# A chunked recurrence beside dense projections: TensorE's order written by the kernel, and an inverse by blocks of 16 in place of 32

## The chip, the cores and the metric

The kernel runs on one core of a Trainium2 chip. The metric is the device time of one execution in microseconds (us), as the median of several runs. A core has TensorE (PE, which multiplies matrices; its weight loads are shown apart as PEld), VectorE (DVE), ScalarE (ACT), GpSimd (POOL) and SyncE (SP, which issues the transfers). Each works through its own list of instructions in order, and semaphores make one wait for another.

## The reference, cut to what matters

The model is a streaming encoder of two layers with D = 1024. It takes 1024 frames of a new stream and 64 frames of a running one. Layer 1 mixes over time with RWKV-7, layer 2 with attention over a sliding window; each is followed by a SwiGLU feed-forward part (FFN). The change lies in the RWKV-7 part, a recurrence with a 64x64 state in each of 16 heads:

```
def step(s, inp):
    r_t, w_t, k_t, v_t, a_t, b_t = inp
    sa = jnp.einsum('bhvk,bhk->bhv', s, a_t)
    s = s * w_t[:, :, None, :] + sa[..., None] * b_t[:, :, None, :] + v_t[..., None] * k_t[:, :, None, :]
    return s, jnp.einsum('bhvk,bhk->bhv', s, r_t)
...
s_fin, y = lax.scan(step, s0.astype(f32), seq_in)
```

After the scan y is normalised per head, a bonus is added, the gate is multiplied in, and the result is projected by w_o. Everything is float32.

## The kernel before

**Tiling.** Tokens are cut into half A (512 frames) and half B (512 frames and the 64 of the running stream, 576 to 580 columns). Features lie on the 128 partitions, 8 tiles of 128. A dense product is made three times over from a high and a low part of each operand: `Dense.mm` (L433 to L435, tile dp) issues high x high, high x low and low x high for each of 8 tiles of the contraction. Weights come in pieces of 512 columns (tile wr); ACT makes the high part (wh, L393), DVE or POOL the low part (wl, L394).

**The recurrence.** It runs in chunks of 64 frames, 17 in all: chunks 0 to 7 beside the r, k and v projections of half B (called stage 1 here), chunks 8 to 16 beside the output projection of half A and its first FFN (stage 2). Both stages are one call of `recur`, the second followed by one for chunk 16. A chunk has four parts, in class `Rwkv`:

- `prep` loads r, k, a and the log decay s, makes scaled copies AR and BK on DVE, ACT and POOL, the norms of the keys (p_rp from c_bd, then tile r_n), the four *triangle groups* (p_rp from r_AR and r_BK, masked by DVE into X, named r_G, L152), and the bonus (tile r_vf).
- `prep2` inverts a triangular 64x64 matrix per head (`inverse`), then copies the rest of X and transposes BK (tile r_BT).
- `chain` is what goes from chunk to chunk: U0 (p_rc from r_sv and r_G), copied by ACT (L283); U (p_rc from r_yc and W), copied by DVE and ACT (L287, L288); the new state (p_rc from r_sv and r_BT, then DVE L301 and L302, tile r_M); and the output Y (p_ry, from r_M and r_AR, then from r_sv and r_G).
- `post` normalises Y, transposes it and stores it (scratch z).

**The inverse.** The 64x64 triangle of each head is seen as two blocks of 32 on the diagonal. ACT copies the diagonal blocks four times over into one tile (L190, 32x1024), so that DVE can solve all heads at once with a row per lane: `for j in range(30, 0, -2)` multiplies (L215) and adds (L219), in up to two halves per step. The two blocks are then joined on TensorE by two groups of 32x32 matmuls (p_rc from r_ixd and r_in, and p_rc from r_ixd alone), each followed by a copy in two halves (L246 on ACT and L247 on DVE; L253 and L254). The result is W, a single buffer.

**What sets the order.** All instructions are handed to a scheduler, which replays them on a model timeline and gives each engine its list. A priority decides between instructions that are ready (low number first). `Two.at(pe, rest)` gives the recurrence's matmuls one priority and its other work another:

```
def recur(chunks, M, base, low):
    rw.two.at(base, base)
    d = rw.prep(chunks[0])
    rw.prep2(d)
    for i, ch in enumerate(chunks):
        ...
            rw.two.at(base + 0.301 + late, low + 0.301 + late)
            nd = rw.prep(chunks[i + 1])
        rw.two.at(base + late, base + late)
        M, Y = rw.chain(ch, d, M)
```

So TensorE's list is the scheduler's. The triangle groups of chunk i+1 come ahead of the chain of chunk i, and its inverse follows behind it.

## Time and profile before

| what | us |
|---|---|
| median of 3 runs | 3048.13 (3044.47 to 3050.98) |
| the profiled execution | 3042.33 |
| its span, from the first to the last instruction | 3040.6 |
| TensorE busy in it | 2854.4 (94%) |
| VectorE busy | 1885.7 (62%) |
| ScalarE busy | 1371.7 (45%) |
| GpSimd busy | 920.5 (30%) |

The profile comes from one execution. Its page gives busy time by engine, the same in 40 slices of 76 us, the clock that TensorE was granted, and the costliest groups of instructions. Views of the trace cut this further: by window, by line, by wait, or in order of time. A float32 matmul of the recurrence that the kernel issues once stands in the trace twice, so "x32" there is 16 of the program. Stage 1 lies at about 265 to 690 us of the span, stage 2 at about 690 to 1192 us.

### The profile page before, as it was taken

The page shows a single profiled execution, that of the slowest core. Times are in us where ns is not written, and L with a number is a line of the kernel's source. Part 1 is how long each engine was busy: PE and PEld are TensorE (multiplying, and loading weights), DVE is VectorE, ACT ScalarE, POOL GpSimd, SP SyncE. Part 2 cuts the span into 40 slices and gives each one's busy share as a digit, 9 for nine tenths or more (in the row PEclk, how much of TensorE's full clock was granted, in tenths as well). Part 3 has the DMA queues.
Part 4 walks back from the last instruction along what each step waited for, and adds up shares of the span by engine and source line. Part 5 has one row for each costly group of instructions (what it writes and reads, how often), then busy time and mean ns, then how long its engine had stood idle before and what let it go on. Part 6 is the DMA issues. An engine that isn't in the chain of part 4 may idle for free. (4 is left out here: it accounts for less than half of the span.)

```text
span 3040.6 us, 51529 instructions
## 1 busy us (share of the span) xinstructions
PE 2854.4 (94%) x19650; PEld 2463.5 (81%) x19650; DVE 1885.7 (62%) x3964; ACT 1371.7 (45%) x2491; POOL 920.5 (30%) x785
## 2 busy tenths in 40 slices
PE   6998888988899999999999999999999999999998
PEld 5677777876677777887789999888777888999998
DVE  8887788968998994357554333565554335533334
ACT  6866665545545542244653222344554233322222
POOL 6555124333333332224211222243111222322221
PEclk9999778988899999999999999999999999999999
DMA  4645353344232225332212222222222332322222
GB/s 145 169 124 148 112 144 93 108 118 133 78 95 88 89 69 137 100 114 80 70 49 63 84 84 84 77 85 79 65 67 74 94 94 80 105 84 84 84 84 70
DMA packets 262048, 289.10 MB, mean 95 GB/s; under 512 B 125029, under 2 KB 143973, under 8 KB 261801
## 3 DMA queue, kind: packets, MB, share of 16 engines
q1 hardware_dynamic: 261800, 285.81, 31.7%
q8 instruction: 154, 2.52, 0.4%
q14 instruction: 94, 0.76, 0.1%
HBM read 243.18 MB, written 41.16 MB: 94 GB/s over the span
## 5 line engine op out<-in xcount | busy, mean ns | idle before, releaser
L433 PE MATMUL dp<-xh,wh 128*128 128x288 f32 (+2 forms) x3480 | 1180.3, 340 | 29.2 <-DVE hx L962 11.4
L434 PE MATMUL dp<-xl,wh 128*128 128x288 f32 (+2 forms) x3480 | 1172.0, 337 | 9.7 <-POOL xl L426 6.5
L435 PE MATMUL dp<-xh,wl 128*128 128x288 f32 (+2 forms) x3480 | 1167.9, 336 | 0.0
L393 ACT CAST wh<-wr 128x512 fp32r<-128x512 f32 x730 | 446.0, 619 | 820.4 <-PE dp L434 613.5
L433 PEld LDWEIGHTS dp<-xh,wh 128*128 128x128 f32 x3480 | 665.6, 192 | 109.9 <-DVE hx L962 16.0
L434 PEld LDWEIGHTS dp<-xl,wh 128*128 128x128 f32 x3480 | 666.0, 191 | 74.6 <-issue 8.6
L435 PEld LDWEIGHTS dp<-xh,wl 128*128 128x128 f32 x3480 | 666.2, 191 | 60.3 <-issue 4.9
L394 POOL TENSOR_TENSOR wl<-wr,wh 128x512 fp32r<-128x512 f32 x243 | 340.2, 1400 | 1063.2 <-ACT wh L393 948.7
L394 DVE TENSOR_TENSOR wl<-wr,wh 128x512 fp32r<-128x512 f32 x487 | 374.6, 772 | 421.1 <-ACT wh L393 417.0
L433 PE MATMUL dp<-mh,wh 128*128 128x288 f32 (+1 forms) x808 | 254.5, 315 | 0.2 <-DVE hx L962 0.2
L435 PE MATMUL dp<-mh,wl 128*128 128x288 f32 (+1 forms) x808 | 254.0, 314 | 0.0
L434 PE MATMUL dp<-ml,wh 128*128 128x288 f32 (+1 forms) x808 | 253.8, 314 | 0.0
L962 DVE TENSOR_TENSOR a_xB<-dp,a_xB 128x288 f32<-128x288 f32 x352 | 157.7, 455 | 83.5 <-PE dp L435 82.8
L943 DVE TENSOR_TENSOR st<-st,dp 128x288 f32<-128x288 f32 (+1 forms) x132 | 70.0, 530 | 222.0 <-PE dp L435 221.6
L945 POOL TENSOR_TENSOR xl<-st,xh 128x288 fp32r<-128x288 f32 (+1 forms) x102 | 102.2, 1002 | 327.6 <-ACT xh L944 318.8
L433 PEld LDWEIGHTS dp<-mh,wh 128*128 128x128 f32 x808 | 152.5, 189 | 10.7 <-issue 3.0
L435 PEld LDWEIGHTS dp<-mh,wl 128*128 128x128 f32 x808 | 152.6, 189 | 8.5 <-issue 2.4
L434 PEld LDWEIGHTS dp<-ml,wh 128*128 128x128 f32 x808 | 152.6, 189 | 6.8 <-issue 1.1
L190 ACT COPY r_f<-r_G 32x1024 f32<-32x1024 f32 x68 | 135.8, 1997 | 37.4 <-DVE r_f L226 25.4
L962 DVE TENSOR_TENSOR hx<-dp,hx 128x512 f32<-128x512 f32 x176 | 119.7, 685 | 47.9 <-PE dp L435 47.3
L215 DVE TENSOR_TENSOR r_f<-r_f,r_f 128x60 f32<-128x60 f32 (+5 forms) x476 | 119.4, 282 | 0.5
L944 ACT CAST xh<-st 128x288 fp32r<-128x288 f32 (+1 forms) x102 | 50.2, 492 | 137.3 <-DVE st L943 136.3
(343 smaller groups left out, 3850.3 us busy)
## 6 DMA issues: line engine op xcount, KB each, us to landing
wr<-in_ffn_in SPq DMA_DIRECT2D x352, 256.0 KB
wr<-in_ffn_out SPq DMA_DIRECT2D x176, 256.0 KB
wr<-in_rkv SPq DMA_DIRECT2D x90, 256.0 KB
wr<-in_rwo SPq DMA_DIRECT2D x32, 256.0 KB
wr<-in_wq SPq DMA_DIRECT2D x32, 256.0 KB
wr<-in_wo SPq DMA_DIRECT2D x32, 256.0 KB
r_r_s<-s_s SPq DMA_DIRECT2D x17, 256.0 KB
r_sv<-s_vt SPq DMA_DIRECT2D x17, 256.0 KB
```

The source lines that it names most:

```text
L190: S.copy(st[32 * q:32 * q + 32].rearrange("p (t g j) -> p t g j", g=4, j=8), src)
L215: V.tensor_tensor(out=Z[:, h, 1:3, r0:4, 0:j], in0=Z[:, h, a, r0:4, j:j + 2].rearrange("p r c -> p c r").unsqueeze(3).broadcast_to([128, 2 ...
L393: nc.scalar.copy(h, x)
L394: (nc.gpsimd if self.turn % 3 == 0 else nc.vector).tensor_tensor(out=l, in0=x, in1=h, op=ALU.subtract)
L433: self.nc.tensor.matmul(ps, lhsT=wh, rhs=xh, start=i == 0, stop=False)
L434: self.nc.tensor.matmul(ps, lhsT=wh, rhs=xl, start=False, stop=False)
L435: self.nc.tensor.matmul(ps, lhsT=wl, rhs=xh, start=False, stop=i == last)
L943: V.tensor_tensor(out=t[o], in0=t[o], in1=p, op=ALU.mult)
L944: S.copy(a.hi[:, q], t[o])
L945: G.tensor_tensor(out=a.lo[:, q], in0=t[o], in1=a.hi[:, q], op=ALU.subtract)
L962: V.tensor_tensor(out=self.x[m][:, q], in0=p, in1=self.x[m][:, q], op=ALU.add)
```

## The change

**TensorE's order.** A new class `Pump` holds the recurrence as a generator. Between `start` and `end` TensorE's list is the order in which the program is written. `Dense.mm` calls `tick` behind each triple of dense matmuls with their columns; `tick` takes 0.44 ns per column and 6 ns from a need, and when the need is used up the next step of the recurrence is issued. Each step yields how much dense work (in ns) is to stand before the next. `burst(6)` issues six steps without dense work between, ahead of the input mixes of r and of k; `drain` issues what is left. The lists of the other engines are still the scheduler's.

**Two chunks ahead.** `prep`, `inverse`, `chain` and `post` are now generators. In `recur`, chunk i's chain is followed by `turns`: the triangle groups, bonus and BK transposes of chunk i+2 alternate with the joins of chunk i+1's inverse.

**Blocks of 16.** The solve on DVE runs `for j in range(14, 0, -2)`, 7 steps in place of 15 and one half in place of two. The copies that spread the blocks are 32x512 in place of 32x1024. Two groups of joins are added on TensorE that make blocks of 32 out of blocks of 16 (p_rc from r_ixd, 32 matmuls of 32x16 each in the program), with a copy on ACT behind the first (L311, tile Q) and an add and a transpose on DVE behind the second (L318, L297). The joins from 32 to 64 stay, 16 matmuls each. W is now written whole, by DVE (L320) and ACT (L321).

```
-        for j in range(30, 0, -2):
+        for j in range(14, 0, -2):
...
-            part = [(h, (j // 4 + 1 - h) // 2) for h in range(2) if (j // 4 + 1 - h) // 2 < 4]
-            for h, r0 in part:
+            r0, n = j // 2, 8 - j // 2
+            V.tensor_tensor(out=Z[:, 1:3, r0:8, 0:j],
...
+            V.tensor_reduce(out=Z[:, b, r0:8, 0:j], in_=Z[:, min(a, 1):min(a, 1) + 3, r0:8, 0:j].rearrange("p c r j -> p r j c"),
+                            axis=AX.X, op=ALU.add)
...
+        for j in range(8):
+            for q in range(4):
+                o = slice(32 * q, 32 * q + 32)
+                self.mm(ps[o, j, :], lhsT=T(q, j, slice(o.start % 64, o.start % 64 + 32)), rhs=XD[o, j, 0:16], start=True, stop=True)
+        S.copy(Q1[:, :, 0:16], ps)
+        yield
...
+                self.mm(ps[o, j, :], lhsT=Q1[o, j, :], rhs=WD[o, j, 16:32], start=True, stop=True)
+        V.tensor_tensor(out=WD[:, :, 16:32], in0=ps, in1=WD[:, :, 16:32], op=ALU.add)
+        turn()
+        V.tensor_scalar(out=W[:, :, 0:32], in0=WD, scalar1=self.e[:, 2:3], scalar2=None, op0=ALU.mult)
+        S.activation(W[:, :, 32:64], WD, AF.Copy, scale=self.e[:, 3:4])
...
+    def tick(self, n):
+
+        if self.gen is None:
+            return
+        self.need -= 0.44 * n + 6
+        while self.gen is not None and self.need <= 0:
+            self.step()
...
+        def turns(g, v, p):
+
+            for gap in (1.2, 1.4, 1.2, 1.4):
+                for x in (g, v):
+                    if x:
+                        step(x, p)
+                        yield gap * scale * us
...
+            k = rw.chain(ch, ds[i], M)
+            step(k, base)
+            if g:
+                step(g, inv)
+            yield 1.8 * scale * us
...
+    pump.start(recur(range(8), M, 1, 2, *FREE[0], {7: lambda M: state.append(M)}), 1)
...
 go(rkv("B", "v", xs["Bv"]), chain(wait(3), take(8 - 3, stage)))
+    pump.burst(6)
     all(r)
     go(rkv("B", "r", xs["Br"]), chain(stage, several(2, take(RING - 8, k))))
+    pump.burst(6)
     all(k)
     all(rkv("B", "k", xs["Bk"]))
-    prio(3)
-    M = recur(range(8, 16), M, 3, LOW[1])
...
+    pump.drain()
...
+    pump.start(recur(range(8, 17), state[0], 3, 4, *FREE[1], {
+        15: saved, 16: lambda M: nc.sync.dma_start(O["wkv_s"], M.rearrange("p a b -> p (a b)"))}), 3)
```

`FREE` gives scale and free time of the two stages: 0.7 and 1.0 us, then 1.0 and 4.0 us. What TensorE finds in its list at three places follows; dp is dense work.

**Place 1: TensorE, the middle of a chunk in stage 1.** Before, U0 of one chunk, a part of its Y and the second join group stand one behind the other between dense matmuls:

```order
L434 MATMUL dp_6690<-xl_6264,wh_6684 128x290
L73 MATMUL p_rc_4160<-r_sv_4155,r_G_3791 64x64 x16
L73 MATMUL p_ry_4159<-r_M_3915,r_AR_3779 64x64 x8
L73 MATMUL p_rc_4044<-r_ixd_4015 32x32 x15
L435 MATMUL dp_6690<-xh_6263,wl_6685 128x290
L433 MATMUL dp_6690<-xh_6270,wh_6684 128x290
L434 MATMUL dp_6690<-xl_6271,wh_6684 128x290
L435 MATMUL dp_6690<-xh_6270,wl_6685 128x290
```

Now the second added join group (tile Q) and the bonus (r_rkr) each stand alone, with nine dense matmuls between them:

```order
L531 MATMUL dp_6126<-xh_4558,wl_6032 128x290
L120 MATMUL p_rc_6194<-r_ixd_5869,Q_2522 32x16 x32
L529 MATMUL dp_6126<-xh_4565,wh_6031 128x290
L530 MATMUL dp_6126<-xl_4566,wh_6031 128x290
L531 MATMUL dp_6126<-xh_4565,wl_6032 128x290
L529 MATMUL dp_6251<-xh_4516,wh_6239 128x290
L530 MATMUL dp_6251<-xl_4517,wh_6239 128x290
L531 MATMUL dp_6251<-xh_4516,wl_6240 128x290
L529 MATMUL dp_6251<-xh_4523,wh_6239 128x290
L530 MATMUL dp_6251<-xl_4524,wh_6239 128x290
L531 MATMUL dp_6251<-xh_4523,wl_6240 128x290
L120 MATMUL p_rp_6260<-r_rkr_5894,c_bd 128x512
```

What moved: a step of the recurrence no longer has another one next to it, but a counted stretch of dense work.

**Place 2: TensorE, stage 1, where the v projection of half B ends and the input of r is mixed.** Before, U, the new state, Y, the key norms and the first triangle group follow each other:

```order
L73 MATMUL p_rc_3521<-r_yc_3519,W 64x64
L817 MATMUL dp_6212<-c_id,st_6052 128x128 x4
L73 MATMUL p_rc_3521<-r_yc_3519,W 64x64 x15
L824 MATMUL dp_6220<-c_id,st_6052 64x128
L73 MATMUL p_rc_3540<-r_sv_3487,r_BT_3397 64x64
L73 MATMUL p_ry_3491<-r_sv_3487,r_G_3123 64x64 x2
L73 MATMUL p_rc_3540<-r_sv_3487,r_BT_3397 64x64 x15
L73 MATMUL p_ry_3491<-r_sv_3487,r_G_3123 64x64 x14
L73 MATMUL p_rp_3756<-c_bd,r_rt_3753 64x2 x8
L73 MATMUL p_rp_3792<-r_AR_3779,r_BK_3780 128x128 x4
```

Now the burst of six steps puts U, a transpose of the chunk before, the new state, Y and a triangle group in a row:

```order
L900 MATMUL dp_4349<-xh_2365,wl_4319 128x290
L915 MATMUL dp_4357<-c_id,st_4027 128x128 x4
L922 MATMUL dp_4365<-c_id,st_4027 64x128
L120 MATMUL p_rc_4370<-r_rt_4233,W 64x64 x16
L124 MATMUL p_ry_3757<-c_id,r_yc_3809 128x128 x4
L120 MATMUL p_rc_4396<-r_sv_4212,r_BT_3439 64x64 x16
L120 MATMUL p_ry_4416<-r_M_3745,r_AR_2894 64x64 x16
L120 MATMUL p_ry_4416<-r_sv_4212,r_G_3169 64x64 x16
L120 MATMUL p_rp_4467<-r_AR_4194,r_BK_4195 128x128
L120 MATMUL p_rp_4468<-r_AR_4194,r_BK_4195 128x128
L120 MATMUL p_rp_4467<-r_AR_4194,r_BK_4195 128x128
```

What moved: the transposes of v (L817 and L824, now L915 and L922) stand ahead of U, and Y is whole behind the new state; in both lists no triple of dense work stands between U and the triangle groups.

**Place 3: TensorE, stage 2, the norm between the output projection of half A and its FFN** (dp from ones and lo: first the sums over features, then their spreading; then the FFN's first matmuls). Before, U0, a join, U, the new state and Y stand around the two matmuls of the norm:

```order
L73 MATMUL p_rc_7630<-r_ixd_7601 32x32
L73 MATMUL p_rc_7746<-r_sv_7741,r_G_7496 64x64 x16
L73 MATMUL p_rc_7630<-r_ixd_7601 32x32 x15
L73 MATMUL p_rc_7775<-r_yc_7773,W 64x64
L532 MATMUL dp_10843<-ones,lo_10553 128x1 x4
L73 MATMUL p_rc_7775<-r_yc_7773,W 64x64 x15
L549 MATMUL dp_10853<-lo_10851,ones 128x512
L73 MATMUL p_rc_7794<-r_sv_7741,r_BT_7651 64x64
L73 MATMUL p_ry_7745<-r_sv_7741,r_G_7496 64x64 x2
L73 MATMUL p_rc_7794<-r_sv_7741,r_BT_7651 64x64 x15
L73 MATMUL p_ry_7745<-r_sv_7741,r_G_7496 64x64 x14
L433 MATMUL dp_10918<-xh_10858,wh_10906 128x512
```

Now only the new state's group stands ahead of them, and the FFN follows at once:

```order
L530 MATMUL dp_8365<-xl_7775,wh_8359 128x512
L531 MATMUL dp_8365<-xh_7774,wl_8360 128x512
L120 MATMUL p_rc_8540<-r_sv_8463,r_BT_7973 64x64 x16
L630 MATMUL dp_8565<-ones,lo_7817 128x1 x4
L647 MATMUL dp_8575<-lo_8573,ones 128x512
L529 MATMUL dp_8640<-xh_8580,wh_8628 128x512
L530 MATMUL dp_8640<-xl_8581,wh_8628 128x512
L531 MATMUL dp_8640<-xh_8580,wl_8629 128x512
```

What moved: Y and the triangle group stand behind the first matmuls of the FFN, where they stood ahead of or among them.

More of the change, by code (lines that the diff above doesn't have):

```diff
@@ new lines, in inverse @@
+        V.tensor_tensor(out=xe[:, :, :, 0], in0=xe[:, :, :, 0], in1=tm, op=ALU.add)
+        XX = Z[:, 2:4].rearrange("p a r s -> p (a r s)")
+        for e in range(2):
+            V.tensor_scalar(out=XX.rearrange("p (r s) -> p r s", r=8)[:, :, 16 * e:16 * e + 16], in0=XL, scalar1=self.e[:, e:e + 1], scalar2=None, op0=ALU.mult)
+        D3 = self.t([128, 2, 8, 32], "ixd")
+        XD, WD = D3[:, 0], D3[:, 1]
+        XO = Z[:, 0:2].rearrange("p a r s -> p (a r s)")
+        V.transpose(out=XO, in_=XX)
@@ L356, in __init__ @@
         self.n = self.turn = 0
-        self.more = self.esb = None
+        self.more = self.esb = self.pump = None
         self.mixed = []
@@ L1074, in tile_stream_step @@
     F = Ffn("A", 0, xA, x0)
-    all(F.main())
+    for _ in F.main():
+        if pump.region and not pump.gen:
+            pump.end()
     rctx.close()
```

325 lines of the change are left out of this document (205 added, 120 removed).

## The prediction

> **What bounds the kernel now.** I read the page's 40 slices first. TensorE's row is full behind slice 16 and has holes ahead of it, where its clock is also below 9:
>
> ```profile
> PE   6998888988899999999999999999999999999998
> DVE  8887788968998994357554333565554335533334
> PEclk9999778988899999999999999999999999999999
> ```
>
> The recurrence lies there. The view by windows, cut at its two stages and its end, gives the amounts:
>
> ```profile
> core 0: us, PE busy (x) PEld busy (x) DVE busy (x) ACT busy (x) POOL busy (x), PEclk, DMA share, GB/s
> 265.00:690.00 425.00, 367.08 (x3685) 323.33 (x3684) 339.46 (x929) 249.48 (x394) 135.47 (x117) 0.86 0.44 122
> 690.00:1192.00 502.00, 454.70 (x3723) 353.90 (x3722) 436.37 (x1090) 243.83 (x340) 178.21 (x139) 0.93 0.30 92
> 1192.00:3040.60 1848.60, 1806.41 (x11191) 1606.41 (x11189) 887.53 (x1676) 689.21 (x1428) 453.84 (x386) 0.99 0.27 83
> ```
>
> TensorE stands idle for 425.0 - 367.1 = 57.9 us in stage 1 and 502.0 - 454.7 = 47.3 us in stage 2, together 105.2 us. While busy it is slowed: 367.1 x 0.14 = 51.4 us and 454.7 x 0.07 = 31.8 us of clock, together 83.2 us. So 188.4 us is all that a better order can win; the 1848.6 us behind are untouched. DVE is busy for 80% and 87% of the stages, and is the next to bound them.
>
> Who ends the idle time is told by the waits of TensorE between 265 and 1192 us (total us, times, longest):
>
> ```profile
> PE p_rc L73 <- ACT r_ixd L246: 13.6, 7, 4.3
> PE p_rp L73 <- ACT r_rt L102: 10.1, 2, 9.1
> PE p_rc L73 <- DVE r_ixd L236: 9.9, 5, 3.5
> PE p_rp L73 <- DVE r_n L110: 6.7, 3, 3.6
> PE dp L433 <- DVE hx L962: 5.7, 4, 2.8
> PE dp L434 <- POOL xl L426: 5.3, 3, 2.9
> ```
>
> There is no one wait: the largest is the copy between the two join groups, then a chunk's beginning, then the end of DVE's solve. How the first comes about is seen in order of time:
>
> ```profile
> 747.89 5.90 ACT L190 COPY r_f<-r_G 32x1024 f32<-32x1024 f32 x3
> 748.09 1.06 PE L73 MATMUL p_rc<-r_ixd,r_in 32*32 32x32 f32 x32 [3.46 <-DVE r_ixd L236]
> 756.88 0.36 ACT L246 COPY r_ixd<-p_rc 32x256 f32<-32x256 f32 x1
> 757.29 0.24 PE L73 MATMUL p_rc<-r_ixd 32*32 32x32 f32 x2 [0.88 <-ACT r_ixd L246]
> 760.30 0.69 PE L73 MATMUL p_rc<-r_ixd 32*32 32x32 f32 x30
> ```
>
> The join ends at 749.15, but its copy of 0.36 us runs at 756.88: ACT first works off what its list has ahead of it, the spreading copies of the next inverse above all.
>
> **The change part by part.**
>
> *Added joins (cost).* Two groups of 32 matmuls in the program, 64 each in the trace, so 128 more per chunk. In the rows above 30 of them take 0.69 us and 2 take 0.24 us: 0.45 / 28 = 16 ns each. 128 x 16 ns = 2.06 us per chunk, 35 us over 17 chunks. Bounds: 0.69 / 30 = 23 ns each gives 50 us; if they fell wholly into time in which TensorE would stand idle, they would cost nothing. I take 35: TensorE is to be filled with dense work around them, so they displace it.
>
> The Trainium skill, "TensorE: Matmul & The Clock Gate", section "Wait — 56ns, not 53.3ns?", says that starts never lie closer than about 25 ns however narrow a matmul is; by that the groups would cost 128 x 25 x 17 = 54 us and the forecast would be 19 us higher. The row of 16 ns says otherwise for matmuls of 32x32, and I go by it.
>
> *Smaller solve (relief of DVE and ACT).* The groups of DVE and ACT that the solve consists of, in both stages:
>
> ```profile
> L190 ACT COPY r_f<-r_G 32x1024 f32<-32x1024 f32 x68 | 135.8, 1997 | 37.4 <-DVE r_f L226 25.4 <-DVE r_G L152 11.4
> L215 DVE TENSOR_TENSOR r_f<-r_f,r_f 128x60 f32<-128x60 f32 (+5 forms) x476 | 119.4, 282 | 0.5
> L219 DVE TENSOR_REDUCE r_f<-r_f 128x30 f32<-128x90 f32 (+5 forms) x476 | 98.7, 237 | 0.5
> L197 DVE TENSOR_TENSOR r_f<-r_f,r_nl 128x1024 f32<-128x1024 f32 x17 | 24.0, 1411 | 0.1
> L207 DVE TENSOR_TENSOR r_f<-c_xl,r_nl 128x256 f32<-128x256 f32 x34 | 23.9, 742 | 0.2
> L195 DVE STREAM_TRANSPOSE r_f<-r_f 128x1024 f32<-128x1024 f32 x17 | 21.1, 1243 | 44.8 <-ACT r_f L190 44.8
> L204 DVE TENSOR_TENSOR r_f<-r_f 128x512 f32<-128x512 f32 x17 | 16.9, 995 | 0.2
> L205 DVE TENSOR_TENSOR r_f<-r_f,r_f 128x512 f32<-128x512 f32 x17 | 15.0, 882 | 0.4
> ```
>
> DVE spends (119.4 + 98.7 + 24.0 + 23.9 + 21.1 + 16.9 + 15.0) / 17 = 18.8 us of a chunk on it. Now: 7 products of 0.28 and 7 sums of 0.24 = 3.6; L197 at a quarter and a scaling like it, 0.7; L195 and L207 at a half, 0.6 + 0.7; L204 and L205 at a quarter, 0.5. That is 6.1 us. Added are two scalings, an add, a transpose and two small products for the norms, six at about 0.4 = 2.4 us. So DVE is relieved of 18.8 - 8.5 = 10 us per chunk, 170 us in all. ACT's four copies go from 2.0 to about 1.0 us each, 4 us per chunk. None of this is on TensorE's list, so in itself it gains nothing; it is what lets idle time go. DVE then needs 339 - 80 = 259 us in stage 1 and 436 - 90 = 346 us in stage 2; TensorE needs 367.1 x 0.86 + 16 = 332 and 454.7 x 0.93 + 19 = 442 us at full clock. So TensorE bounds both stages, DVE at 78% of it.
>
> *TensorE's order (gain, with new waits).* Now each step waits behind a counted stretch of dense work, and if its input is late, that dense work's successors are queued behind it. The cover follows from the start times of the first and last of 47 and of 7 consecutive dense matmuls:
>
> ```profile
> 324.60 0.30 PE L434 MATMUL dp<-xl,wh 128*128 128x290 f32 x1
> 330.76 0.30 PE L435 MATMUL dp<-xh,wl 128*128 128x290 f32 x1
> 754.62 0.39 PE L435 MATMUL dp<-xh,wl 128*128 128x512 f32 x1
> 756.02 0.40 PE L435 MATMUL dp<-xh,wl 128*128 128x512 f32 x1
> ```
>
> 6.16 / 46 = 134 ns in stage 1, 1.40 / 6 = 233 ns in stage 2. Six to twelve of them between steps (place 1 shows nine) are 0.8 to 1.6 us, six to nine in stage 2 are 1.4 to 2.1 us. What has to be done in that time:
>
> ```profile
> L283 ACT COPY r_yc<-p_rc 128x512 f32<-128x512 f32 x17 | 10.0, 586 | 16.4 <-PE p_rc L73 15.7 <-PE p_ry L77 0.5
> L287 DVE COPY r_sv<-p_rc 64x512 f32<-64x512 f32 x17 | 11.6, 680 | 4.2 <-PE p_rc L73 3.9
> L301 DVE TENSOR_TENSOR r_M<-p_rc,r_M 128x512 f32<-128x512 f32 x17 | 11.6, 685 | 5.7 <-PE p_rc L73 5.7
> L302 DVE TENSOR_TENSOR r_M<-r_M,r_PC 128x512 f32<-128x512 f32 x17 | 11.7, 685 | 0.1
> L394 DVE TENSOR_TENSOR wl<-wr,wh 128x512 fp32r<-128x512 f32 x88 | 67.2, 766 | 4.0 <-ACT wh L393 3.7
> ```
>
> A copy is 0.6 to 0.7 us, the state 1.4 us; with one weight split of 0.77 us caught ahead of it, 1.4 to 2.1 us. In stage 1 about half of a chunk's dozen handovers then fall short by some 0.3 us: 2 us per chunk, 16 in all; in stage 2 about a quarter: 1 us per chunk, 9. Beside the chunks: the mixes of r and k, where dense work waits for new inputs and the burst has no cover (place 2), 10 us (today's waits on the mixes, xl L426 at their head, come to about that); the start, 4; and the norm of place 3:
>
> ```profile
> 761.93 0.69 DVE L898 TENSOR_TENSOR hx<-dp,hx 128x512 f32<-128x512 f32 x1
> 764.80 1.86 PE L532 MATMUL dp<-ones,lo 128*128 128x1 f32 x8
> 768.48 2.07 PE L549 MATMUL dp<-lo,ones 128*128 128x512 f32 x2
> 772.93 0.96 PE L433 MATMUL dp<-xh,wh 128*128 128x512 f32 x3
> ```
>
> From the last add of the projection to the FFN's first matmul are 11.0 us. U0, U, the state and Y filled part of it; now only the state's group (1.1 us) and the norm's own 3.9 us do. That leaves 6 to 7 us idle: 7. Left idle: 16 + 9 + 10 + 4 + 7 = 46 us. Bounds: none, if each cover holds; today's 105.2, if the same queues end every step.
>
> *Clock.* Today 83.2 us are lost to it for 105.2 us of idle time, 0.79 us per us. For 46 us I take 36 us. It isn't tied to idle time alone:
>
> ```profile
> 372.20:389.20 17.00, 16.84 (x102) 12.94 (x101) 12.54 (x20) 13.71 (x17) 7.27 (x8) 0.50 0.58 148
> ```
>
> Here TensorE was busy for 16.84 of 17.00 us, with triangle groups, joins and transposes close together, and had half the clock. Spreading them among dense work speaks for less than 36, the remaining holes for as much.
>
> *Sum.* 105.2 + 83.2 - 35 - 46 - 36 = 71 us. 3040.6 - 71 = 2969.6 us of span. The profiled execution is 1.7 us above its span, and the median of the runs 5.8 us above that execution: 2977 us.
>
> **The rivals.**
>
> A, *the covers hold* (0.12). 10 us idle and 8 of clock are left: 188.4 - 35 - 18 = 135, so 2913 us. For it: a copy of 0.36 to 0.7 us under 0.8 us or more. Against it: the rows at 747 to 757 us, where a free copy came 7.7 us late behind its own list.
>
> B, *the clock stays up although holes remain* (0.10). Holes of a few tenths among dense work leave it whole: the 36 us fall away, 2941 us. Against it stands the window at 372. The Trainium skill, "TensorE: Matmul & The Clock Gate", section "Why this matters for your kernels", asks only that no idle time exceed about 3 us between bursts; by that rule alone this rival would hold. In the window at 372 us there was no such idle time and the clock was 0.50, so the trace does not agree.
>
> C, *stage 1 stays at the pace of DVE and ACT* (0.15). Covers of 0.8 us are too short, stage 1 keeps its idle time and clock and pays 16 us for joins; stage 2 gains 47.3 + 31.8 - 19 - 16 - 13 = 31 us. Gain 15, so 3033 us. For it: stage 1 is where DVE has most to do per dense matmul; against it: the 80 us taken from DVE.
>
> D, *slower* (0.09). TensorE's fixed list makes it stand at its turn where the scheduler's list had something ready, as at place 3. Idle time and clock remain as they are, and the joins come on top: 3048 + 35 = 3083 us. It decides from the point where 1.79 x idle exceeds 188.4 - 35 = 153 us: 86 us idle, 5 us per chunk. Against it: it would need each second handover to miss by close to a microsecond.
>
> E, *no change within 0.2%* (0.04): left idle near 86 us.
>
> **How the numbers follow.** My forecast, 2977 us, has 0.50, with 2945 to 3010 as its own range (left idle 30 to 60 us, joins 16 to 23 ns). Faster by over 0.2% (which is about what a measurement of this kernel can tell from no change) hold it, A, B and C: 0.87. Same: 0.04. Slower: 0.09. From 2920 to 3035 us leaves out D, nearly all of A and little else, about 0.2.
>
> **What would show it.** Right: idle time of TensorE below 60 us and a clock of 0.92 or more in the first stage, 0.96 in the second; DVE's solve at 8 to 9 us per chunk; both added join groups at 1.0 to 1.3 us; stage 1 about 390 us long, stage 2 about 470. A hole of 6 us at the norm. Wrong: the clock in stage 1 at 0.86 as now; waits of TensorE on r_ixd, Q or r_sv of over 5 us per chunk (D); DVE busy for over 90% of a stage (C); the small matmuls at 25 ns.

## The result: 0.7% slower, outside the predicted range

| | before | changed |
|---|---|---|
| median of 4 runs, us | 3046.36 | 3067.47 |
| ratio, 95% interval | | 1.0068 (1.005 to 1.0085) |
| span of the profiled execution, us | 3040.6 | 3069.8 |

The forecast was 2977 us (2920 to 3035). The 40 slices of the changed kernel, in the page:

```profile
PE   6898878788898999999999999999999999999998
DVE  8787377846878864356654333565554335633334
PEclk9998878888899999999999999999999999999999
```

DVE has gaps now where it was full, as forecast, but TensorE's holes in slices 4 to 15 have not closed. The view by windows of the changed kernel, cut at its own two stages (length, then the busy time of PE, PEld, DVE, ACT and POOL, then the granted clock):

```profile
265.00:700.00 435.00, 364.41 (x4644) 319.38 (x4643) 282.47 (x606) 210.29 (x375) 126.23 (x108) 0.85 0.43 117
700.00:1192.00 492.00, 433.20 (x4865) 331.45 (x4865) 369.29 (x756) 210.36 (x327) 171.63 (x143) 0.93 0.32 93
```

TensorE stands for 70.6 us of the first stage and 58.8 us of the second, 129.4 us together. The clock is 0.85 and 0.93 (0.86 and 0.93 before), where 0.92 and 0.96 were forecast.

Since the recurrence moved against the dense work, the two kernels are compared between the same two dense matmuls, the 447th and the 3346th of each (188.7 to 1249.6 us before, 191.0 to 1277.2 us now; behind them lie the same stretches again). "Clock" is busy time times the clock that was missing, "work" is busy time times the clock:

| us | length | idle | clock | work |
|---|---|---|---|---|
| before | 1060.9 | 109.2 | 83.2 | 868.6 |
| changed | 1086.2 | 136.4 | 82.5 | 867.2 |

So the loss is idle time, 27 us more. Work is the same, although 128 matmuls per chunk were added. A ledger is of one execution, and executions of one kernel differ in the clock above all: the granted clock of the changed kernel's four lies between 0.961 and 0.963, that of six of one variant below between 0.959 and 0.965, and 0.001 is 3 us. So a difference of some 10 us in the clock between two ledgers means little by itself.

What TensorE waits for between 266 and 1226 us (us, times, longest):

```profile
PE p_rc L120 <- DVE r_sv L366: 19.8, 9, 3.8
PE p_rc L120 <- DVE r_iqt L330: 17.6, 13, 3.6
PE p_rc L120 <- DVE r_ixd L297: 14.6, 4, 5.8
PE p_rp L120 <- DVE r_G L219: 8.4, 2, 8.1
PE p_rc L120 <- ACT r_sv L367: 6.9, 10, 2.1
PE p_ry L120 <- POOL r_by L385: 6.6, 7, 2.2
```

The copies of U (r_sv, 26.7 us on both engines) and the copy behind the third join group (r_iqt) lead. One of these waits in order of time:

```profile
934.83 1.15 PE L120 MATMUL p_rc<-r_rt,W 64*64 64x64 f32 x32
...
937.44 0.77 DVE L200 TENSOR_SCALAR r_n<-p_rp 32x32 f32<-32x32 f32 x4
937.55 0.40 PE L531 MATMUL dp<-xh,wl 128*128 128x512 f32 x1
938.24 0.45 DVE L297 STREAM_TRANSPOSE r_ixd<-r_ixd 128x256 f32<-128x256 f32 x1
938.61 0.31 DVE L202 RECIPROCAL r_n<-r_n 128x32 f32<-128x32 f32 x1
938.96 0.21 DVE L204 STREAM_TRANSPOSE r_n<-r_n 128x32 f32<-128x32 f32 x1
939.20 0.69 DVE L1041 TENSOR_TENSOR st<-st,dp 128x512 f32<-128x512 f32 x1
939.81 0.23 DVE L205 TENSOR_SCALAR r_nl<-r_n,lanes 128x16 f32<-128x16 f32 x1
939.94 0.69 DVE L490 TENSOR_TENSOR wl<-wr,wh 128x512 fp32r<-128x512 f32 x1
940.54 0.23 DVE L206 SCALAR_TENSOR_TENSOR r_nl<-r_n,lanes,r_nl 128x16 f32<-128x16 f32 x1
940.69 0.68 DVE L366 COPY r_sv<-p_rc 64x512 f32<-64x512 f32 x1
...
941.42 0.33 PE L120 MATMUL p_rc<-r_sv,r_BT 128*64 128x64 f32 x2 [3.47 <-DVE r_sv L366]
```

U ends at 935.98. The cover holds until 937.95, longer than the copy of 0.68 us needs. But the copy starts at 940.69, since DVE's list has the norms of a later chunk, the end of a solve, an add of the FFN and a weight split ahead of it, and DVE works through them without a pause. Over the 17 chunks the copy on DVE starts 1.95 us behind the end of U on average and 5.1 us at worst, the one on ACT 3.20 us; the cover, from the end of U to where TensorE would start the state, is 2.0 us at the median.

The copies were no sooner before the change. One chunk of the kernel before, in order of time:

```profile
973.58 1.03 PE L73 MATMUL p_rc<-r_yc,W 64*64 64x64 f32 x28
...
979.34 0.67 DVE L287 COPY r_sv<-p_rc 64x512 f32<-64x512 f32 x1
...
982.60 0.27 PE L73 MATMUL p_rc<-r_sv,r_BT 128*64 128x64 f32 x1
```

U ends at 974.61, its copy starts 4.73 us later, and the state's first matmul, at 982.60, does not wait for it. Over the 17 chunks the copies of the kernel before start 2.37 us (DVE) and 3.36 us (ACT) behind the end of U, a little later than now. But the scheduler's list has 3.8 us at the median between U and the state, and TensorE waited for these copies only 2.7 us in all:

```profile
PE p_rc L73 <- DVE r_sv L287: 2.2, 3, 1.0
PE p_rc L73 <- ACT r_sv L288: 0.5, 3, 0.2
```

So at U the change did not make the copies late; it made the cover shorter than a lateness that was there already. The 24 us more at U (26.7 for 2.7) are nearly all of the 27 us; the other waits changed places and came to about the same sum.

### The profile page after: what moved, and what is told of

Same layout as the page of the kernel before. It is cut to its first block, busy times and chain, and to the rows that moved or that the text cites. A ratio compares the mean times of both kernels' runs of the same rounds, so it can differ in the third digit from the quotient of the medians.

```text
span 3069.8 us, 55274 instructions
## 1 busy us (share of the span) xinstructions
PE 2852.1 (93%) x21826; PEld 2453.6 (80%) x21826; DVE 1762.9 (57%) x3326; ACT 1305.7 (43%) x2471; POOL 905.3 (29%) x786
## 5 line engine op out<-in xcount | busy, mean ns | idle before, releaser
L529 PE MATMUL dp<-xh,wh 128*128 128x288 f32 (+2 forms) x3480 | 1203.7, 346 | 27.5 <-ACT xh L521 8.4
L490 POOL TENSOR_TENSOR wl<-wr,wh 128x512 fp32r<-128x512 f32 x243 | 332.2, 1367 | 1070.4 <-ACT wh L489 981.7
L490 DVE TENSOR_TENSOR wl<-wr,wh 128x512 fp32r<-128x512 f32 x487 | 366.6, 756 | 489.4 <-ACT wh L489 484.8
L1039 ACT ACTIVATE st<-dp 128x288 f32<-128x288 f32 (+1 forms) x132 | 62.2, 471 | 93.2 <-PE dp L531 92.8
L522 POOL TENSOR_TENSOR xl<-st,xh 128x512 fp32r<-128x512 f32 (+2 forms) x37 | 65.9, 1788 | 76.2 <-ACT xh L521 76.2
```

The costliest lines, as they stand in the source:

```text
L490: (nc.gpsimd if self.turn % 3 == 0 else nc.vector).tensor_tensor(out=l, in0=x, in1=h, op=ALU.subtract)
L522: (eng or self.nc.vector).tensor_tensor(out=lo, in0=x, in1=hi, op=ALU.subtract)
L529: self.nc.tensor.matmul(ps, lhsT=wh, rhs=xh, start=i == 0, stop=False)
L1039: S.activation(t[o], p, AF.Silu)
```

## The experiments

Each is named by what it changes; ratios are to the kernel before, with 95% intervals, and the ledger is taken as above.

### Which half of the change costs

*The smaller inverse alone.* The kernel before with `inverse` and the norms of the changed one, without its `yield`s; TensorE's order stays the scheduler's.

> The kernel before, whose TensorE order stays the scheduler's, with the inverse by blocks of 16 alone. My theory (the loss comes from TensorE's fixed order in front of lists of DVE and ACT that the scheduler still orders; the inverse in itself helps): DVE is relieved by about 8 us a chunk, the joins cost 21 us, TensorE's idle time between 258 and 1198 us falls from 107 to about 80 us, and the time is 3030 us (3010 to 3046). Rival (the two added joins with their handovers are the loss): idle time rises, 3070 us or more.

Measured: 3051.14 us, ratio 1.0019 (1.0008 to 1.003). Idle 81.6 us, clock 102.9 us, work 881.2 us. Both theories were wrong on the time. The inverse does what was forecast for idle time (28 us less) and its joins cost work (13 us more), but the clock takes 20 us back:

```profile
265.00:690.00 425.00, 386.54 (x4696) 340.87 (x4695) 298.12 (x623) 219.95 (x393) 132.73 (x115) 0.86 0.47 130
690.00:1192.00 502.00, 462.38 (x4865) 369.03 (x4865) 362.56 (x746) 205.80 (x320) 167.47 (x141) 0.90 0.31 91
```

The second stage is busier than before (462 against 455 us) at a lower clock (0.90 against 0.93). By the granted clock of all ten executions of this kernel, against the 13 of the kernel before that ran beside them, the clock's loss grew by about 11 us; the 20 us of the two ledgers overstate it. From here to the changed kernel the fixed order adds 55 us of idle time, gives back 20 us of clock and saves 14 us of work. So the fixed order with its two chunks ahead loses 16 of the 21 us, from 3051 to 3067. The fixed order with the old inverse was not run, so what it would do alone is open.

### The triangle groups, a gain that the prediction missed

Work did not grow because the triangle groups' work, at full clock, fell from 67 to 39 us while that of the joins rose by 21: a half group of triangles became nearly twice as fast. Before, in order of time (8 in the trace are 4 of the program, all of one half of the heads):

```profile
845.17 1.16 PE L73 MATMUL p_rp<-r_AR,r_BK 64*128 64x128 f32 x8
```

and now, 16 with the halves taking turns:

```profile
906.24 1.16 PE L120 MATMUL p_rp<-r_AR,r_BK 64*128 64x128 f32 x16
```

*The turns taken back in the changed kernel.*

```
-            for i in range(4):
-                for par in range(2):
+            for par in range(2):
+                for i in range(4):
```

> The changed kernel, with the 16 triangle matmuls of a half group sorted: four with the even heads (upper 64 rows of the operands), then four with the odd heads, as the scheduler had them in the kernel before; now they take turns. My theory: turns let two neighbours run side by side, which is why a triangle matmul costs 71 ns at full clock in the changed kernel and 123 ns before. Then the 544 of them go back from 39 to about 67 us and the time from 3067 to 3095 us (3085 to 3110). Rival: the groups became cheap because dense work lies between them, whatever the order inside: 39 us and 3067 us as now.

Measured: 3106.02 us, ratio 1.0194 (1.0177 to 1.0211), 39 us more than the changed kernel. Work 882.4, clock 95.7, idle 139.7 us: 15 of work, 13 of clock and 3 of idle time between the two profiled executions, which lie 31 us apart. The theory holds, its size was 17 us of the triangles' own time in place of 28; a group of 16 takes

```profile
492.09 1.81 PE L120 MATMUL p_rp<-r_AR,r_BK 64*128 64x128 f32 x16
```

1.81 us, less than two times 1.16. The Trainium skill, "TensorE: Matmul & The Clock Gate", section "Why this matters for your kernels", says that matmuls over fewer than 128 rows run at the same time when their operands lie in different groups of rows. That 16 fit into the time of 8 agrees.

*The turns alone, in the kernel before:* each triangle matmul is ordered behind the one of the other half.

```
+                    if i or par:
...
+                        self.tc.add_manual_dep(x.ins, last.ins.name, info, reason="turns")
+                    last = x
```

> The kernel before, with one order between neighbours added: even and odd heads take turns in the triangle groups; all else is the scheduler's. My theory: the 544 triangle matmuls go from 67 to about 39 us at full clock and the time from 3046 to 3018 us (3005 to 3028). Rival (dense work between the groups made them cheap): no change, 3046 us.

Measured: 3061.04 us, ratio 1.0049 (1.0034 to 1.0064). Work falls by 21 us, where 28 were expected, but idle time rises by 35 us: with turns both banks have to be free before the group starts, and TensorE's wait for the mask that empties them (r_G) goes from 1.6 to 13.5 us, that for r_sv from 2.7 to 16.0 us. Under the scheduler's order the gain is lost in new waits.

### The late copies

*The norms behind U.* The step `step(g, inv)` of the key norms moves from ahead of U to behind it.

> The changed kernel, with the step of the key norms (p_rp from c_bd, and DVE's L200 to L206 behind it) issued behind U in place of ahead of it. My theory (copies stand in DVE's list behind other work): of the 33 us that the copies of U queue on DVE, the 12 us of the norms go, TensorE's wait for r_sv falls from 27 to about 15 us, and the time to 3052 us (3040 to 3062). Rival (the cover is too short for the copy itself): the wait falls only by the microsecond that the norm's matmuls now add to the cover and comes back between U0 and U; 3065 us or more.

Measured: 3065.46 us, ratio 1.0064 (1.0047 to 1.0081).

```profile
PE p_ry L120 <- POOL r_by L385: 16.8, 14, 3.2
...
PE p_rc L120 <- DVE r_sv L366: 4.6, 4, 1.7
```

The wait for r_sv on DVE falls by 15 us, but the wait for GpSimd's empty step between the halves of Y rises from 6.6 to 16.8 us. Theory and rival both hold in part: the copy on DVE starts 1.45 us behind U in place of 1.95, and the norms' matmuls make the cover 2.8 us at the median in place of 2.0. The time did not follow, since the wait moved one step down the chain.

*The joins' copies at the chain's priority.* `step(x, p if x is g else base)` in `turns`.

> The changed kernel, with the steps of the inverse's joins (their copies on DVE and ACT) at the priority of the chain instead of that of the side work. My theory: the copy of the third join on DVE (r_iqt, L330), which queues 74 us in all behind the next chunk's preparation, comes sooner; TensorE's wait for it falls from 17.6 to below 6 us and the time to about 3050 us (3040 to 3062). Rival (waits move): what is put behind is late next (r_sv, r_ixd, the dense inputs), 3067 us, within 6.

Measured: 3075.87 us, ratio 1.0093 (1.0068 to 1.0117).

```profile
PE p_rc L120 <- DVE r_iqt L330: 18.2, 14, 3.6
```

Neither theory: the wait itself did not move. A priority only decides between instructions that are ready on the scheduler's timeline. The likely reading, which no run shows by itself, is that the copy already stood where the model sees its group end, and that the chip's DVE comes there late.

*The copy on another engine.* `V.tensor_copy(QT[96:128], ...)` becomes `S.copy(...)`.

> The changed kernel, with both halves of the copy behind the third join group (r_iqt) on ACT, where the one half came at once, in place of one on ACT and one on DVE, where the other queued 4.4 us on average. A priority did not move it, so my theory is now that the list is right for the scheduler's model and DVE runs behind that model; then only another engine or less work helps. TensorE's wait for r_iqt falls from 17.6 to below 4 us, idle time from 129 to about 112, and the time to about 3042 us (3032 to 3054). Rival (waits are conserved: what comes off here is waited for at the next step): 3062 us or more.

Measured: 3056.54 us, ratio 1.0051 (1.0033 to 1.0069). The wait for r_iqt is gone, and idle time is what it was, 136.3 us: the rival's waits, conserved (that for r_sv on DVE rose from 19.8 to 27.5 us). Eleven us were gained all the same. The ledger puts them down to the clock (66.2 against 82.5 us), but the six executions scatter from 3054 to 3068 us with a granted clock of 0.965 to 0.959, 0.963 on average against 0.962 for the changed kernel; where the 11 us come from is not shown.

*DVE's work reduced:* the loop of seven steps left out.

> The changed kernel without the seven steps of the solve on DVE (L276 and L279; the inverse is left unfinished, so the values are not the reference's): DVE has 4 us of a chunk less. My theory (lists of DVE lag): TensorE's waits for DVE's r_sv, r_iqt and r_ixd together fall from 52 to below 30 us, and the time to about 3035 us (3020 to 3050). Rival (DVE's load does not matter to the waits, since it is busy for only 65 and 75% of the stages): 3067 us, within 8.

Measured: 3045.22 us, ratio 0.9999 (0.9984 to 1.0014). Waits for r_sv and r_ixd on DVE go from 34 to 13 us, r_iqt stays at 16.7. Of the 22 us, 12 are at r_ixd, the result of the solve itself, which comes sooner without its steps. The other 10 are at r_sv, whose copy now starts 1.09 us behind U: there DVE's load sets the wait, although DVE is busy for only 65 and 75% of the changed kernel's stages.

*Longer covers:* `FREE = ((0.85, 1.0), (1.5, 4.0))`.

> The changed kernel with longer stretches of dense work between the steps: scale 0.85 for 0.7 in stage 1, 1.5 for 1.0 in stage 2. My theory (copies come late by up to 5 us because DVE and ACT lag behind the lists that the scheduler made, so a longer cover hides more of it): TensorE's idle time from the start of stage 1 to the first FFN falls from 129 to about 95 us, most of it in stage 2, and the time to about 3030 us (3015 to 3050). Rival (the scheduler orders DVE and ACT against the same longer model time, other work moves into the longer covers, and the copies are as late as before): 3067 us, within 8.

Measured: 3048.69 us, ratio 1.0007 (0.9996 to 1.0018). Idle 126.5, clock 65.1 us. Half of the 37 us expected, about half of it by clock. U's copy on DVE still queues for 1.7 us (1.95 in the changed kernel): longer covers hide lateness and don't cure it.

*Three repairs at once:* norms behind U, joins' copies at the chain's priority, the first half of Y issued with the new state so that r_by has the state's cover.

> The changed kernel with three repairs of its late handovers: the key norms behind U, the joins' copies at the chain's priority, and the first half of Y issued with the new state, so that GpSimd's empty step between the halves of Y (r_by) has the state's cover. My theory: waits for r_sv, r_iqt and r_by fall from 51 to below 25 us, and with 0.6 us of clock per us the time goes to about 3030 us (3015 to 3050). Rival (waits move to the next input of the chain): 3060 us or more.

Measured: 3042.7 us, ratio 0.9996 (0.9983 to 1.0009). r_sv and r_by fall to 8.7 us together, r_iqt stays at 17.3. The two repairs shown above gave 2 us and -8 us alone; with r_by mended as well the gain is 25 us. That a chain of handovers has to be mended link by link fits this; the repair of Y was not run alone, so how much of the 25 us is its own is open.

### What makes the clock drop

The clock is granted in stretches of 3.41 us: in each trace, its changes between 266 and 1226 us lie multiples of 3.413 us apart, to 2 ns. The view by windows at the wait shown above, cut at these stretches:

```profile
934.83:938.24 3.41, 3.12 (x43) 2.45 (x42) 3.07 (x13) 0.00 (x0) 0.00 (x0) 1.00 0.21 75
938.24:941.66 3.42, 0.24 (x2) 0.19 (x2) 3.35 (x9) 1.72 (x2) 1.04 (x1) 1.00 0.00 0
941.66:945.07 3.41, 1.36 (x26) 1.27 (x26) 1.50 (x3) 2.02 (x4) 0.31 (x2) 0.50 0.40 123
945.07:948.49 3.42, 3.42 (x19) 2.73 (x16) 1.79 (x3) 0.00 (x0) 2.15 (x2) 0.50 0.34 115
948.49:951.90 3.41, 3.41 (x29) 2.50 (x27) 2.11 (x5) 1.20 (x2) 0.26 (x2) 1.00 0.20 76
```

TensorE stands for 3.2 us of one stretch at full clock; the next is granted half; it has 2 us of standing too, so the one after is slow again although TensorE is busy throughout, and only then is the clock back. Over the stretches between 266 and 1226 us in all 20 traces, the share that was slow, by how long TensorE had stood in the stretch ahead:

| stood in the stretch ahead | it was at full clock | it was slow |
|---|---|---|
| under 0.8 us | 1% of 3818 | 40% of 720 |
| 0.8 to 1.2 us | 7% of 230 | all 55 |
| 1.2 to 1.8 us | 46% of 247 | all 93 |
| over 1.8 us | 97% of 283 | all 159 |

So the loss is a threshold, and sticky: holes that stay under 0.8 us in a stretch cost only themselves, 2 us of them cost a stretch or more at half speed. What ends a slow period is not shown: behind a slow stretch 40% stayed slow with hardly any standing. The prediction's window at 372 us is such a period, and it is among the 29 of 3818 that began without standing, so it stays unexplained. The Trainium skill, "TensorE: Matmul & The Clock Gate", section "Why this matters for your kernels", asks that no gap exceed about 3 us. The gap of 3.47 us above is over that, but less was enough: of 147 stretches at full clock with over 1.8 us of standing and no single gap of 3 us, 142 were followed by a slow one.

*Useless work in the holes.* Two matmuls of 128x512 ahead of the state's group and of the fourth join group, into the bank that the group overwrites.

> The changed kernel with useless work in its two commonest holes: two matmuls of 128x512 (about 1 us together, into the bank that the next group overwrites) ahead of the state's group and ahead of the fourth join group, 34 us in all. They wait for nothing, so where TensorE would stand for r_sv or r_iqt they fill the first microsecond. In the runs so far a 3.4 us stretch of the clock was slow in nearly all cases when TensorE had stood for over 1.8 us of the stretch ahead, and hardly ever when for under 0.8 us. If that is the cause, slow time falls from 195 to below 160 us although work was added; of 34 us some 20 fill idle time, and the time comes to 3067 + 14 - 18 = about 3063 us (3050 to 3075). Rival (the clock is lowered by the amount of work of the recurrence, as the run with the scheduler's order and the smaller inverse seems to say, 27 us less idle and 20 us more clock loss): slow time stays or grows, 3080 us or more.

Measured: 3097.56 us, ratio 1.0175 (1.0155 to 1.0195). Slow time falls from 195 to 150 us and the clock's loss from 82.5 to 65.8 us, while work grows by 58 us (1.7 us per pair, not 1.0, which is why the time missed). All four executions have a clock of 0.965 to 0.968, against 0.961 to 0.963. More work and a better clock: the rival falls, and standing is what starts most slow periods. Why the smaller inverse alone lost clock with less idle time is not explained by this: its slow periods are about as many as before (24 and 23), but last longer (9.2 against 8.5 us), and 31 of its 55 stretches behind a slow one stayed slow with under 0.8 us of standing.

### Why DVE runs behind its list

In the changed kernel 121 of DVE's 1380 operations between 266 and 1226 us take much longer than their like (over 1.3 times the median of the same line and shape, and 0.1 us more), 96 us in all. The extreme is a copy of 8 columns; the view by line of the changed kernel gives its shortest, median and longest time in ns:

```profile
L173 DVE COPY r_PC<-r_rt x17: 113/172/1276, 271.2 to 1043.0; 128x8 f32<-128x8 f32 x17
```

In order of time, that copy beside a product of GpSimd:

```profile
432.74 2.39 POOL L406 TENSOR_TENSOR r_vf<-r_vf,r_g 128x512 f32<-128x512 f32 x1 [2.00 <-DMA r_g<-s_g]
...
433.89 1.28 DVE L173 COPY r_PC<-r_rt 128x8 f32<-128x8 f32 x1
435.08 0.75 DVE L522 TENSOR_TENSOR xl<-st,xh 128x580 fp32r<-128x580 f32 x1
```

It ends about when GpSimd's product ends. All 121 lie beside a product of GpSimd, as only 379 of the 1380 do. The Trainium skill, "SBUF — State Buffer", section "SBUF: two separate sides", describes a port pair that GpSimd and some of DVE's operations hold in turn, the other standing until the instruction ends; the rows agree.

*GpSimd's share left out:* five products per chunk (L189, L190, L405 to L407).

> The changed kernel without five of GpSimd's products per chunk (L189, L190, L405 to L407: the bonus loses two factors, the output its gate, weight and bias, so the values are not the reference's); DVE's own work stays. In the trace of the changed kernel 113 operations of DVE in the recurrence take much longer than their like, 91 us in all, and every one of them lies beside a GpSimd product; 42 of the 91 us beside these five. My theory (DVE runs behind its list because it is held up beside GpSimd, and that is why copies are late): the extra time falls to about 50 us, the waits for r_sv, r_iqt and r_ixd from 59 to about 40 us, and the time to about 3048 us (3036 to 3058). Rival (the lists are late for other reasons): 3067 us, within 6.

Measured: 3020.49 us, ratio 0.9924 (0.9905 to 0.9942). The extra time falls to 47 us in 56 operations, idle time to 109.4 and the clock's loss to 56.8 us:

```profile
265.00:690.00 425.00, 363.60 (x4702) 317.22 (x4700) 268.28 (x617) 217.45 (x388) 77.65 (x71) 0.89 0.46 126
690.00:1192.00 502.00, 461.43 (x5023) 355.02 (x5024) 352.46 (x769) 218.58 (x339) 119.87 (x105) 0.96 0.34 99
```

The gain is 47 us where 20 were expected.

*The same five products on DVE,* `G.tensor_tensor` becoming `V.tensor_tensor`; nothing is left out.

> The changed kernel with the same five products on DVE, so that nothing is left out: DVE gets 5 x 0.69 = 3.4 us of a chunk more and loses 2.5 us of hold-up. Theory: nearly even, 3067 us or a little more (3060 to 3080). Rival (only DVE's amount of work counts): 58 us more of DVE's work make the copies later by as much as the seven steps left out made them earlier, 3085 us or more.

Measured: 3037.8 us, ratio 0.9975 (0.9964 to 0.9986): 30 us faster than the changed kernel, though DVE has more to do. The rival that GpSimd's own results simply come sooner explains little: TensorE's waits put down to GpSimd fall from 13.7 to 9.5 us, those put down to DVE from 78.8 to 67.7. Under this order the hold-up weighs more than the amount, which counts too: the 17 us between this run and the one that left the products out.

*The same move in the kernel before.*

> The kernel before (scheduler's order, blocks of 32) with the same five products of GpSimd on DVE. In its trace 141 slow operations of DVE take 115 us longer than their like, 45 of them beside these five; DVE is busy for 84% of the recurrence and gets 58 us more. If the hold-up beside GpSimd costs any order alike, it gains too: 3030 us (3020 to 3040). If a fixed order of TensorE is what makes late copies dear (the scheduler's order hides them, and DVE's amount counts there), it is the same or slower: 3044 to 3065 us. I expect the second.

Measured: 3059.04 us, ratio 1.005 (1.0035 to 1.0065). DVE's extra time falls from 117 to 66 us there too, but the kernel is 14 us slower, idle 121.0 us. So the move does not pay under every order: with the scheduler's order and a DVE busy for 84% of the recurrence, its amount seems to count more.

### Versions that beat both kernels

*Repaired:* norms behind U, Y's first half with the state, both copies of the third join on ACT, covers (0.85, 1.0) and (1.4, 3.0), and 4 to 6 us more ahead of the first norms, of the second chunk and of a stage's last output. Then with covers (0.8, 1.0) and (1.1, 4.0). Then with 0.75 in stage 1 and 2 us ahead of the last output, since the first version stood for 21 us at the end of its first stage.

> The changed kernel with the repairs that worked, together: key norms behind U, first half of Y with the state, both copies of the third join on ACT, covers of 0.85 and 1.4 (free 1.0 and 3.0), 4 to 6 us more ahead of the first norms, the second chunk and the last output of each stage. If the repairs add up: idle time from 129 to about 85 us, slow clock from 195 to about 150 us, and 3012 us (2995 to 3028), faster than both kernels. Rival (they share their gain, since one slow window of the clock covers several waits): 3035 us.

> As tuned, with covers of 0.8 and 1.1 (free 1.0 and 4.0), so that the last chunks of stage 2 still have FFN work beside them at nearly the pace of the changed kernel. If length of cover is what counts, it is 5 to 15 us slower than tuned; if the drawn-out end of stage 2 costs what the covers gain, as fast or faster.

> The repaired kernel with stage 1 at 0.75 in place of 0.85 and 2 us in place of 6 ahead of a stage's last output. In the repaired kernel the end of stage 1 shows two holes, 8.9 us in its last output and 12.1 us at the first mixes of the output projection, which need that output. If they come from the stretched stage, they fall to about 8 us together and the time from 3019 to about 3005 us (2998 to 3015). Rival (shorter covers in stage 1 give the same back at the handovers): 3019 us, within 5.

Measured: 3019.09 us (0.9917, 0.9903 to 0.9932), 3019.46 us (0.9918, 0.9897 to 0.9939) and 3015.78 us (0.9902, 0.9888 to 0.9917). The repairs together gain 48 to 52 us on the changed kernel: idle 107.7, 106.6 and 100.6 us, clock 53.4, 64.7 and 58.5 us. The first two do not differ: covers of 1.4 or 1.1 in stage 2 decide nothing here. In the third the two holes at the end of stage 1 fell from 21 us to under 5, as expected, but the time by 3 us only: the rival holds, and most of it came back elsewhere. The copies of U on DVE come no sooner in these versions than in the changed kernel (1.9 to 2.0 us behind U). What differs is the cover of U: with the norms behind U it is 3.2 to 4.0 us at the median, near the 3.8 of the kernel before.

*Repaired, with five and with seven products on DVE* (L164 and L417 too).

> The repaired kernel (3016 us) with the five products on DVE. Alone the move gave 30 us, the repairs 51 us. If they add up, 2990 us (2980 to 3000). If both take away the same late copies, 3005 to 3015 us.

> As tuned_dve, with the two other full products of the recurrence (the scaled keys, L164, and the norm of Y) on DVE as well: DVE gets 1.4 us of a chunk more and GpSimd keeps only the power, the empty steps and the splits for the dense work. If hold-up decides, 5 us faster than with five; if DVE's amount begins to, slower by as much.

Measured: 3013.31 us (0.9895, 0.9879 to 0.9912) and 3015.67 us (0.9909, 0.9889 to 0.9929). The move adds 2.5 us to the repairs, within the intervals, so the hold-up and the late copies are largely one loss, seen from two sides. Hold-up alone costs little where the covers are long: the version without the move has 143 slow operations of DVE, 110 us of extra time, more than the changed kernel, and is 52 us faster. The best version's windows:

```profile
265.00:670.00 405.00, 346.51 (x4604) 302.63 (x4603) 276.73 (x633) 210.71 (x380) 81.77 (x67) 0.88 0.42 118
670.00:1192.00 522.00, 486.47 (x5164) 376.41 (x5165) 397.40 (x826) 236.60 (x371) 136.65 (x111) 0.96 0.35 105
```

Stage 2 has the clock that the prediction wanted (0.96). Stage 1, where half the idle time left is in the dense work's own waits, has not (0.88).

## Why the prediction was wrong, step by step

**What bounds the kernel: right.** The stages' idle time and clock were where time was to be won; everything behind them came out the same to 2 us.

**Added joins: mis-sized.** 35 us were forecast, 16 ns each. The joins' work went from 24.5 to 45.8 us, 21 us more. The new groups are half as wide, and 64 of them take

```profile
867.37 0.73 PE L120 MATMUL p_rc<-r_ixd,Q 32*32 32x16 f32 x64
```

0.73 us, 11 ns each, outside "1.0 to 1.3 us". The sign of being wrong, 25 ns each, did not come either.

**Smaller solve: right in kind, too large.** Forecast 8.5 us of a chunk, measured 13.1 with the norms' two scalings.

```profile
L276 DVE TENSOR_TENSOR r_f<-r_f,r_f 128x28 f32<-128x28 f32 (+3 forms) x119 | 40.2, 337 | 3.0
L279 DVE TENSOR_REDUCE r_f<-r_f 128x14 f32<-128x42 f32 (+3 forms) x119 | 27.8, 234 | 3.1
L253 ACT COPY r_f<-r_G 32x512 f32<-32x512 f32 x68 | 74.4, 1095 | 19.7 <-DVE r_G L219 19.1
```

The seven steps (4.0 against 3.6 us) and ACT's copies (1.1 against 1.0 us each) were well sized. The rest, put at 4.9 us with its scalings, took 9.1. DVE's busy time in the two stages fell by 124 us (339.5 + 436.4 to 282.5 + 369.3) in place of 170.

**TensorE's order: the step that failed.** "A copy is 0.6 to 0.7 us, the state 1.4 us; with one weight split of 0.77 us caught ahead of it, 1.4 to 2.1 us." The copies' durations were right, and so were the covers, 2.0 us at U. But a copy had not one split ahead of it, it had a queue: U's copy starts 1.95 us behind the end of U on DVE and 3.20 us on ACT, on average, before it has run at all. So 129.4 us were left idle in the two stages in place of 46. The trace of before held the number: there the copies of U started 2.37 and 3.36 us late, and only the 3.8 us of other work behind U hid it. The prediction had a warning in its own rows, ACT's copy that came 7.7 us late, and quoted it against rival A, but its sum took one split. It trusted that DVE, with less to do, would be on time. DVE had less to do and ran late all the same, in part because it was held up beside GpSimd. Its average load could not show this.

**Clock: wrong with the idle time.** 36 us were worked out as a price per us of idle time. Measured 82.5. The price is a threshold per stretch and a period that outlasts its cause, so it cannot be scaled: the changed kernel has 27 us more idle time than the one before and the same loss of clock.

**A term that was missing.** The triangle groups' turns saved 15 us of work and 13 of clock in the run that took them back. They stood in the order shown at place 2, where a row of four on one tile became turns between two tiles, and the prediction read them as a matter of place only.

**The norm at place 3: right, or nearly.** Forecast 6 to 7 us.

```profile
794.13 1.87 PE L630 MATMUL dp<-ones,lo 128*128 128x1 f32 x8 [2.69 <-DVE lo L622]
797.29 2.08 PE L647 MATMUL dp<-lo,ones 128*128 128x512 f32 x2 [1.29 <-DVE lo L640]
801.48 0.79 PE L529 MATMUL dp<-xh,wh 128*128 128x512 f32 x1 [2.12 <-ACT xh L521]
803.42 0.80 PE L530 MATMUL dp<-xl,wh 128*128 128x512 f32 x1 [1.15 <-DVE xl L522]
```

2.69 + 1.29 + 2.12 + 1.15 = 7.3 us.

**The rivals.** D was nearest to what happened: TensorE stands at its turn while the copy it needs is queued. It gave 3083 us with idle time and clock as before and 35 us of joins; measured were 27 us more idle time, the same clock, and joins paid for by the triangle groups: near in the sum, by luck, and off in the terms. It had 0.09 because "it would need each second handover to miss by close to a microsecond"; 19 of the 34 copies of U made TensorE wait, by 1.4 us on average. Its sign, over 5 us per chunk at r_ixd, Q or r_sv, did not come: they are 2.5 us per chunk, a third of the 7.6 us per chunk that the stages stood. B was right on the clock for the holes it named, a few tenths, but the holes left were longer, and 2 us in a stretch do not leave it whole. A falls, since the covers did not hold, and C, since stage 2 gained nothing (58.8 us idle for 47.3).

## What to carry to other kernels

An order fixed on one engine is only as good as the lists of the engines that feed it: before fixing it, measure for each handover, in the trace of the kernel before, how long the copy stands in its engine's queue behind the end of its input, not how long the copy takes, and how much other work the old list had in that time. A raised priority did not move a late copy here; another engine, less work, less hold-up or a longer cover did, and a mended wait tends to turn up at the next handover. Read an order for what stands next to what inside a group, too: matmuls over half the rows took nearly half the time when the halves took turns.

## What the runs showed of the hardware that had not been expected

- Whether a stretch of 3.41 us has the full clock goes by how long TensorE stood in the stretch ahead: behind one at full clock 1% were slow after less than 0.8 us, 97% after more than 1.8 us; behind a slow one 40% stayed slow even after less than 0.8 us.
- A DVE copy of 8 columns took 1276 ns beside a GpSimd product, 172 ns at the median. Five products moved from GpSimd to DVE made the changed kernel 30 us faster and the kernel before 14 us slower.
- 64 matmuls of 32x32 by 16 columns take 0.73 us together, 11 ns each; their starts lie 1 to 32 ns apart.
